# Shift and scale of the first block: dot products on VectorE replaced by TensorE products with row blocks of w_ada

## The chip, the cores and the metric

The kernel runs on one core of a Trainium2 chip. The metric is the device time of one execution in microseconds (us). Three runs of the kernel before gave 1245.27 us (median; lowest 1242.26, highest 1246.87). One further execution was profiled; it took 1246.47 us, of which 1244.7 us are the span from the first to the last recorded instruction, and the rows below come from it.

## The reference

Two transformer blocks run one after the other on 256 tokens of width 1024, all in float32. Only the start of the first block is touched here:

```python
c_act = jax.nn.silu(c)                       # c: 1 x 1024
mod = c_act @ w_ada[l] + b_ada[l]            # 6144 numbers
shift1, scale1, gate1, shift2, scale2, gate2 = jnp.split(mod, 6, axis=-1)

h = modulate(x, norm_mix_g[l], shift1, scale1)   # rmsnorm(x, g) * (1 + scale1) + shift1
proj = h @ w_in[l]                               # 256 x 1024 times 1024 x 4096
```

So `shift1` and `scale1` are the first 2048 columns of `c_act @ w_ada`, and no product with `w_in` can start before some of them are known. After that come attention, a pooling mixer, a merge, the expert layer (16 experts of each of 8 heads gathered per token from two tables of 16384 rows) and a second block with two attentions and a gated feed-forward layer. None of these is changed.

## The kernel before

**Layout.** Activations of the first stage are kept feature-major: `xT` is 128 partitions x 8 feature blocks x 256 tokens. A weight passes through `Weights` (lines 28 to 85): a list of 512 KB blocks in the order in which they are used, read by SyncE's queue into a ring of seven `raw` buffers, and, where the block is marked for it, split by ScalarE (`hi`, line 53) and VectorE (`lo`, line 54) into two parts, of which six are kept. `mm3` (line 138) makes one float32 product from three TensorE products of the parts (lines 139 to 141). A read of a new block into the ring waits until the buffer's last reader is done.

**The order.** The program is written out by hand: each engine executes its instructions in the order in which the code issues them. `FIRST` names six column groups of `w_in` whose products are made in two rounds, `g = 0` with the features 0 to 511 and `g = 1` with 512 to 1023, so that the first round needs shift and scale of half the features only. Each round has 6 blocks and 144 matmuls.

**The first phase.** `c` is read twice, as a column (`c_col`) and broadcast to all partitions (`c_all`, line 278). The host hands in `w_ada_t`, the transposed first 2048 columns of `w_ada`. `mod_dot` (line 391) takes 128 rows of it, and VectorE multiplies them by `c_all` and adds up along the row (line 394): one instruction of 1024 columns gives 128 numbers of shift or scale as one column of `modc`. Eight dots precede each round. Meanwhile ScalarE squares `xT` (line 388), TensorE adds the squares (line 307), ScalarE and VectorE make the reciprocal root (312, 313), TensorE spreads it over the partitions (316), and VectorE multiplies `xT` by it to `xn` (486). The bias is added (488), `A1 = (1 + scale) * g` is formed (489), and `affine_split` (430) makes `hh` on ScalarE (434) and `hl` on VectorE (435, 428), the two parts of `h`. Between the rounds `keep_clock` (143) issues 14 matmuls that nobody reads.

**Later columns.** The other 4096 columns of `w_ada` are already made on TensorE, spread over the following stage: `modulation` (398) multiplies `c_rep` (c in 32 equal columns) by row blocks, four column groups in four 32-row strips of one bank (line 407), and `mod_columns` (416) turns the resulting rows into columns by transposes (419).

Of the kernel before, what the change touches and what calls it, by code (L numbers as in the profile page):

```python
# [7 lines left out]
F32 = mybir.dt.float32  # L8
# [100 lines left out]
def fused_blocks_kernel(ctx: ExitStack, tc: tile.TileContext, a, out: bass.AP):  # L109
# [10 lines left out]
    def slot3(tag, name, a_, dt=F32):  # L120
        return slot(tag, name, dt).rearrange("p (a b) -> p a b", a=a_)
# [42 lines left out]
    def add_dot(n):  # L164
        W["dot", n] = block(a["w_ada_t"][n * 128:(n + 1) * 128].rearrange("p (o f) -> p o f", o=1), (1, 1024), False)
# [11 lines left out]
    for g in range(2):  # L177
        for kc in range(4 * g, 4 * g + 4):
            add_dot(8 + kc)
            add_dot(kc)  # L180
        for j in FIRST:
            in_block(j, g)
# [93 lines left out]
    ada_buf = slot3("A", "ada_buf", 2)  # L276
    c_all, ada_out = ada_buf[:, 0], ada_buf[:, 1]
    nc.sync.dma_start(c_all, a["c"].to_broadcast([128, D]))
    xT = slot3("B", "xT", KC)
    nc.sync.dma_start(xT, a["x_t"])  # L280
    vcol = const.tile([128, 76], F32, name="vcol")
    nc.sync.dma_start(vcol, a["cols1"])
    ws.prefetch(6)
    ident = const.tile([128, 128], F32, name="ident")
    nc.scalar.dma_start(ident, a["ident"])
    es = ExitStack()
# [10 lines left out]
    nc.scalar.activation(ada_out, c_all, AF.Sigmoid)  # L297
    nc.vector.tensor_tensor(c_all, c_all, ada_out, op=OP.mult)
    nc.scalar.activation(c_col[:, 1], c_col[:, 0], AF.Sigmoid)
    G_MIX, P_SCALE, G_FFN, G_FIN = 48, 56, 60, 68  # L300
# [87 lines left out]
    nc.scalar.activation(sq, xT, AF.Square)  # L388
    xn = slot3("F", "xn", KC)

    def mod_dot(n):

        w = ws.get(W["dot", n], 1)
        nc.vector.scalar_tensor_tensor(ada_out, w[:, 0], 1.0, c_all, op0=OP.mult, op1=OP.mult, accum_out=modc[:, n:n + 1])
# [3 lines left out]
    def modulation():  # L398

        for g in (1, 2):  # L400
            mp = pp.tile([128, 512], F32, tag="o", name="mp")
            for kc in range(KC):
                for half in range(2):
# [10 lines left out]
                    yield  # L414

# [39 lines left out]
    h_parts = parts(hh, hl)  # L455
    first_ps = [mm_tile(), mm_tile()] + [pp.tile([128, 512], F32, tag=tag, name="first_ps", bufs=bufs)
# [18 lines left out]

    for g in range(2):
        ks = slice(4 * g, 4 * g + 4)
        for kc in range(4 * g, 4 * g + 4):
            mod_dot(8 + kc)
            mod_dot(kc)  # L480
            if kc == 2:
                sq_ps = aux_tile()
                square_sums(sq_ps, sq, range(KC))
                rs = rstd_rows(sq_ps, rstd)
            if kc in (3, 4):
                nc.vector.tensor_tensor(xn[:, ks], xT[:, ks], rs[:, None, :].to_broadcast([128, 4, 256]), op=OP.mult)
        for c0 in (4 * g, 8 + 4 * g):
            nc.vector.tensor_tensor(modc[:, c0:c0 + 4], modc[:, c0:c0 + 4], vcol[:, c0:c0 + 4], op=OP.add)
        nc.vector.scalar_tensor_tensor(A1[:, ks], modc[:, 8 + 4 * g:12 + 4 * g], 1.0,
                                       vcol[:, G_MIX + 4 * g:G_MIX + 4 * g + 4], op0=OP.add, op1=OP.mult)  # L490
# [807 lines left out]
```

## Time and profile before

| | us |
|---|---|
| median of three runs | 1245.27 |
| the profiled execution | 1246.47 |
| its span | 1244.7 |
| TensorE busy in the span | 1064.2 (86%) |
| VectorE busy | 845.4 (68%) |
| ScalarE busy | 462.0 (37%) |
| GpSimd busy | 536.0 (43%) |

The share of an engine is an average over stages with different limits. From about 220 to 880 us gathers of the expert rows fill the transfers at some 409 GB/s; before that and after it TensorE is busy almost without a break. The change lies in the first 65 us, so the reading has to be made there. "Granted clock" is the share of the full TensorE clock as the profile gives it for a stretch; how fast the engine really steps is seen from the distance between the starts of equal matmuls.

### The profile page before, as it was taken

Reading aid. Unit: us, or ns where it says so; the run is one execution under the profiler, and the core shown is the slowest. Engines: PE = TensorE matmul, PEld = TensorE weight load, DVE = VectorE, ACT = ScalarE, POOL = GpSimd, SP = SyncE. Lnnn points to the kernel's source line nnn. Section 1 sums busy time; section 2 is a strip of 40 time slices with the busy share of each in tenths; the row PEclk is TensorE's granted clock in tenths of the full one; section 3 lists DMA queues with packets and bytes.
Section 4 is the critical chain, followed back from the end, with each engine's and each line's share of the span. In section 5 each row is a group of like instructions: output and inputs, shape, how many; then the busy total and the mean of one; then the engine's idle time right before and its main releaser. Section 6 shows DMA issues by size and latency. Waiting matters only on the chain.

```text
span 1244.7 us, 15745 instructions
## 1 busy us (share of the span) xinstructions
PE 1064.2 (86%) x5328; PEld 707.2 (57%) x5328; DVE 845.4 (68%) x1846; ACT 462.0 (37%) x887; POOL 536.0 (43%) x569
## 2 busy tenths in 40 slices
PE   4999999698889978776877777777899989999996
PEld 4977899554444423222322222222388879999995
DVE  6864475886876677668766776674356568777776
ACT  4345544323333322221322212221246464655552
POOL 0111001667677777677677777777511310000001
PEclk9999999799999999999999999999999999999998
DMA  9998984799999999999999999999986453656530
GB/s 346 330 315 307 321 284 153 278 346 406 409 386 392 407 408 409 409 409 409 358 409 409 409 409 409 409 409 409 347 289 185 153 186 123 197 181 194 183 123 34
DMA packets 161104, 390.59 MB, mean 314 GB/s; under 512 B 12472, under 2 KB 83648, under 8 KB 160768
## 3 DMA queue, kind: packets, MB, share of 16 engines
q0 software_dynamic: 74864, 272.27, 55.6%
q1 hardware_dynamic: 85520, 116.33, 28.4%
q8 instruction: 43, 0.70, 0.2%
q10 hardware_dynamic: 640, 0.98, 0.2%
q14 instruction: 37, 0.30, 0.1%
HBM read 388.22 MB, written 1.06 MB: 313 GB/s over the span
## 4 chain that ended last, share of the span: by engine, by line
PE 37%; DMA 27%; DVE 12%; POOL 9%; issue 9%; ACT 4%; SPq 0%; DVEq 0%; POOLq 0%; ACTq 0%
DMA urows<-in_peer_u_dram,ex 19%; PE mm L139 7%; PE mm L141 7%; PE mm L140 7%; DMA vrows<-in_peer_v_dram,ex 5%; POOL vrows L806 5%; DVE dot L905 5%; POOL urows L806 5%; PE acc L919 3%; PE down L141 2%; PE down L139 2%; PE down L140 2%; DVE lo L54 1%; PE mp L407 1%; ACT hi L53 1%
## 5 line engine op out<-in xcount | busy, mean ns | idle before, releaser
L919 PE MATMUL acc<-vrows,dg 128*128 128x512 f32 x1024 | 491.5, 612 | 127.9 <-ACT dg L916 89.6
L905 DVE SCALAR_TENSOR_TENSOR dot<-urows,h2rows 128x1024 f32<-128x1024 f32 x256 | 312.0, 1219 | 173.7 <-DMA urows<-in_peer_u_dram,ex 172.3
L919 PEld LDWEIGHTS acc<-vrows,dg 128*128 128x128 f32 x1024 | 178.8, 190 | 420.7 <-issue 228.6
L806 POOL DMA_INDIRECT vrows<-in_peer_v_dram,ex x256 | 242.6, 948 | 103.8 <-issue 60.5
L806 POOL DMA_INDIRECT urows<-in_peer_u_dram,ex x256 | 241.7, 944 | 93.2 <-issue 65.4
L54 DVE TENSOR_TENSOR lo<-raw,hi 128x1024 fp32r<-128x1024 f32 (+1 forms) x152 | 182.0, 1222 | 89.6 <-ACT hi L53 88.0
L916 ACT ACTIVATE dg<-ident,wgt 128x128 f32<-128x128 f32 x256 | 96.0, 397 | 252.2 <-PE acc L919 246.7
L53 ACT CAST hi<-raw 128x1024 fp32r<-128x1024 f32 (+1 forms) x152 | 154.0, 1045 | 34.1 <-DMA raw<-in_w_in_dram 25.8
L139 PE MATMUL mm<-xh,hi 128*128 128x256 f32 x480 | 137.0, 285 | 2.2 <-ACT vab L1021 2.2
L140 PE MATMUL mm<-xl,hi 128*128 128x256 f32 x480 | 136.7, 285 | 0.0
L141 PE MATMUL mm<-xh,lo 128*128 128x256 f32 x480 | 135.6, 283 | 0.0
L139 PEld LDWEIGHTS mm<-xh,hi 128*128 128x128 f32 x480 | 91.1, 190 | 5.1 <-ACT vab L1021 2.5
L140 PEld LDWEIGHTS mm<-xl,hi 128*128 128x128 f32 x480 | 91.1, 190 | 0.4
L141 PEld LDWEIGHTS mm<-xh,lo 128*128 128x128 f32 x480 | 91.3, 190 | 0.0
L1120 POOL TENSOR_TENSOR r<-r,ln 128x512 f32<-128x512 f32 x2 | 3.0, 1488 | 195.2 <-ACT r L1119 195.2
L1176 DVE SCALAR_TENSOR_TENSOR u<-mm,col,u 128x255 f32<-128x255 f32 x88 | 42.4, 482 | 33.7 <-ACT u L1173 32.1
L337 POOL TENSOR_SCALAR p<-p,mnsm 128x128 f32<-128x128 f32 (+1 forms) x24 | 20.2, 851 | 91.1 <-DVE mnsm L335 79.2
L139 PE MATMUL mm<-hh,hi 128*128 128x256 f32 x160 | 47.6, 298 | 5.2 <-ACT hi L53 5.2
L852 POOL TENSOR_TENSOR h2T<-xT,rs 128x1024 f32<-128x1024 f32 x2 | 4.7, 2352 | 107.2 <-ACT rs L847 107.2
L1173 ACT ACTIVATE u<-mm,col 128x256 f32<-128x256 f32 x44 | 24.9, 566 | 59.1 <-PE mm L141 32.4
L141 PE MATMUL mm<-hh,lo 128*128 128x256 f32 x160 | 46.3, 289 | 0.5 <-DVE lo L54 0.5
L930 ACT ACTIVATE wgt<-act 128x8 f32<-128x8 f32 x32 | 6.6, 208 | 106.8 <-DVE dot L905 106.7
(345 smaller groups left out, 1778.5 us busy)
## 6 DMA issues: line engine op xcount, KB each, us to landing
raw<-in_w_in_dram SPq DMA_DIRECT2D x45, 512.0 KB, 6.0
raw<-in_w_up_dram SPq DMA_DIRECT2D x44, 512.0 KB, 4.3
raw<-in_w_ada_dram SPq DMA_DIRECT2D x32, 512.0 KB, 5.2
raw<-in_w_down_dram SPq DMA_DIRECT2D x22, 512.0 KB, 4.0
raw<-in_w_ada_t_dram SPq DMA_DIRECT2D x16, 512.0 KB, 8.2
raw<-in_w_out_dram SPq DMA_DIRECT2D x16, 512.0 KB, 4.9
raw<-in_peer_wq_dram SPq DMA_DIRECT2D x8, 512.0 KB, 5.6
urows<-in_peer_u_dram,ex POOLq DMA_INDIRECT x256, 8.0
```

The lines of the kernel that those rows point to most:

```text
L53: self.nc.scalar.copy(hi, raw)
L54: self.nc.vector.tensor_tensor(lo, raw, hi.bitcast(F32), op=OP.subtract)
L139: nc.tensor.matmul(o, lh, rh, start=first, stop=False)
L140: nc.tensor.matmul(o, lh, rl, start=False, stop=False)
L141: nc.tensor.matmul(o, ll, rh, start=False, stop=last)
L337: eng.tensor_scalar(neg[:, s], neg[:, s], sm[:, i:i + 1], None, op0=OP.mult)
L806: nc.gpsimd.indirect_dma_start(out=g, out_offset=None, in_=tables[kind], in_offset=bass.IndirectOffsetOnAxis(ap=experts[unit][:, k:k + 1], ...
L905: nc.vector.scalar_tensor_tensor(dot, u, 1.0, h2rows, op0=OP.mult, op1=OP.mult, accum_out=act[:, half * HK + k:half * HK + k + 1])
L916: nc.scalar.activation(dg, ident, AF.Copy, scale=wgts[prev][:, k:k + 1])
L919: nc.tensor.matmul(acc[:, s], dg, v[:, s], start=prev == ((prev[0][0], 0), 0) and k == 0, stop=prev == ((prev[0][0], NH - 1), 1) and k == ...
L1173: nc.scalar.activation(dst, src, AF.Identity, bias=ccol[:, 3, c + f:c + f + 1], scale=ccol[:, 2, c + f:c + f + 1])
L1176: nc.vector.scalar_tensor_tensor(dst[:, n:], src[:, :256 - n], ccol[:, 2 - n, c + f:c + f + 1], dst[:, n:], op0=OP.mult, op1=OP.add)
```

## The change

Shift and scale of the first block are made the way the later columns were: `first_products` multiplies `c_rep` by row blocks of `w_ada` itself. A block holds 128 rows of `w_ada` and, for one half of the features, 512 columns of shift and 512 of scale; its two matmuls go to two 32-row strips of one bank, and eight blocks add up to the result for a half. `first_columns` copies the two strips out, turns them into columns by four transposes, adds the bias and forms `A1`. The first half's products stand ahead of round 0, mixed with the sums of squares; the second half's stand inside round 0, behind the groups 4, 5 and 6. `c` is no longer broadcast by a read; `c_rep` is made at the start on GpSimd. `x` is read and squared in two halves. `vcol` and `ident` are read by ScalarE's queue. Ahead of round 1 there are 5 unread matmuls in place of 14.

```diff
+    def add_first_ada(g, kc):
+
+        rows = a["w_ada"][0][kc * 128:(kc + 1) * 128, 0:2048].rearrange("p (o h f) -> p o h f", o=2, h=2)
+        W["ada", 0, kc, g] = block(rows[:, :, g], (2, 512), False)
...
     for g in range(2):
-        for kc in range(4 * g, 4 * g + 4):
-            add_dot(8 + kc)
-            add_dot(kc)
+        for kc in range(KC):
+            add_first_ada(g, kc)
         for j in FIRST:
             in_block(j, g)
...
-    ada_buf = slot3("A", "ada_buf", 2)
-    c_all, ada_out = ada_buf[:, 0], ada_buf[:, 1]
-    nc.sync.dma_start(c_all, a["c"].to_broadcast([128, D]))
     xT = slot3("B", "xT", KC)
-    nc.sync.dma_start(xT, a["x_t"])
-    vcol = const.tile([128, 76], F32, name="vcol")
-    nc.sync.dma_start(vcol, a["cols1"])
-    ws.prefetch(6)
+    x_halves = slice(0, 4), slice(4, 8)
+    for ks in x_halves:
+        nc.sync.dma_start(xT[:, ks], a["x_t"][:, ks])
...
+    ws.prefetch(7)
...
-    nc.scalar.activation(ada_out, c_all, AF.Sigmoid)
-    nc.vector.tensor_tensor(c_all, c_all, ada_out, op=OP.mult)
     nc.scalar.activation(c_col[:, 1], c_col[:, 0], AF.Sigmoid)
+    nc.vector.tensor_tensor(c_col[:, 0], c_col[:, 0], c_col[:, 1], op=OP.mult)
+    c_rep = tmp.tile([128, KC, 32], F32, name="c_rep", bufs=1)
+    nc.gpsimd.tensor_copy(c_rep, c_col[:, 0, :, None].to_broadcast([128, KC, 32]))
...
-    nc.scalar.activation(sq, xT, AF.Square)
+    for ks in x_halves:
+        nc.scalar.activation(sq[:, ks], xT[:, ks], AF.Square)
...
+    def first_products(g, mp, kcs):
+
+        for kc in kcs:
+            w = ws.get(W["ada", 0, kc, g], 1)
+            for j in range(2):
+                nc.tensor.matmul(mp[32 * j:32 * j + 32, :], c_rep[:, kc, :], w[:, j, :],
+                                 start=kc == 0, stop=kc == KC - 1, tile_position=(0, 32 * j))
+
+    def first_columns(g, mp, mt):
+
+        row = tmp.tile([128, 512], F32, tag="modrow", name="modrow", bufs=1)[0:64]
+        nc.vector.tensor_copy(row, mp[0:64])
+        for b in range(4):
+            nc.tensor.transpose(mt[:, b * 64:(b + 1) * 64], row[:, b * 128:(b + 1) * 128], ident[0:64, 0:64])
...
+        nc.vector.tensor_tensor(both, v, vcol[:, 0:16].rearrange("p (j b) -> p j b", j=2)[:, :, ks], op=OP.add)
+        nc.vector.scalar_tensor_tensor(A1[:, ks], modc[:, 8 + 4 * g:12 + 4 * g], 1.0,
+                                       vcol[:, G_MIX + 4 * g:G_MIX + 4 * g + 4], op0=OP.add, op1=OP.mult)
...
+    sq_ps, first_mp = aux_tile("sums"), aux_tile("first_mp")
+    square_sums(sq_ps, sq, range(0, 4))
+    first_products(0, first_mp, range(0, 3))
+    square_sums(sq_ps, sq, range(4, 8))
+    first_products(0, first_mp, range(3, 6))
+    rs = rstd_rows(sq_ps, rstd)
+    first_products(0, first_mp, range(6, KC))
+    first_columns(0, first_mp, pp.tile([128, 512], F32, tag="s", name="mt", bufs=2))
+    for ks in x_halves:
+        nc.vector.tensor_tensor(xn[:, ks], xT[:, ks], rs[:, None, :].to_broadcast([128, 4, 256]), op=OP.mult)
...
+    first_mp = aux_tile("first_mp")
+    FIRST_ADA = {4: (0, 1, 2), 5: (3, 4, 5), 6: (6, 7)}
     for g in range(2):
         ks = slice(4 * g, 4 * g + 4)
-        for kc in range(4 * g, 4 * g + 4):
-            mod_dot(8 + kc)
-            mod_dot(kc)
-            if kc == 2:
-                sq_ps = aux_tile()
-                square_sums(sq_ps, sq, range(KC))
-                rs = rstd_rows(sq_ps, rstd)
-            if kc in (3, 4):
-                nc.vector.tensor_tensor(xn[:, ks], xT[:, ks], rs[:, None, :].to_broadcast([128, 4, 256]), op=OP.mult)
...
-            nc.vector.tensor_tensor(c_col[:, 0], c_col[:, 0], c_col[:, 1], op=OP.mult)
-            c_rep = tmp.tile([128, KC, 32], F32, name="c_rep", bufs=1)
-            nc.vector.tensor_copy(c_rep, c_col[:, 0, :, None].to_broadcast([128, KC, 32]))
...
+            if g == 0 and j in FIRST_ADA:
+                first_products(1, first_mp, FIRST_ADA[j])
+                if j == 6:
+                    first_columns(1, first_mp, aux_tile("mt"))
             if g == 0 and j == FIRST[-1]:
-                keep_clock(aux_tile(), hh, 14)
+                keep_clock(aux_tile(), hh, 5)
```

On TensorE the start of the program reads so, before (-) and now (+). `aux` and `sums` hold the sums of squares, `first_mp` the products with `w_ada` (two matmuls for a block), `mt` the transposes.

```order
-L307 MATMUL aux<-ones,sq 128x1 x16
-L316 MATMUL aux<-ident,rstd 128x128 x2
+L308 MATMUL sums<-ones,sq 128x1 x8
+L418 MATMUL first_mp<-raw,c_rep 32x512 x6
+L308 MATMUL sums<-ones,sq 128x1 x8
+L418 MATMUL first_mp<-raw,c_rep 32x512 x6
+L317 MATMUL sums<-ident,rstd 128x128 x2
+L418 MATMUL first_mp<-raw,c_rep 32x512 x4
+L426 MATMUL mt<-ident,modrow 128x64 x4
```

Sixteen matmuls and four transposes have come to stand between the sums and the first product with `w_in`, and the second half of the sums now stands behind the first six of them.

On VectorE, around the first use of `A1` (shown as `A_113`), the program before has these rows; `ada_buf` is written by the dots.

```order
L394 SCALAR_TENSOR_TENSOR ada_buf,modc<-raw,ada_buf 128x1024 x6
L313 RECIPROCAL rstd<-rstd 128x2
L394 SCALAR_TENSOR_TENSOR ada_buf,modc<-raw,ada_buf 128x1024 x2
L486 TENSOR_TENSOR xn<-xT,aux 128x1024
L488 TENSOR_TENSOR modc<-modc,vcol 128x4 x2
L489 SCALAR_TENSOR_TENSOR A_113<-modc,vcol 128x4
L435 TENSOR_SCALAR mtmp<-xn,A_113,modc 128x256 x2
```

The changed program has these at the same place (`A1` is `A_116`); `modrow` is the copy of the two strips.

```order
L314 RECIPROCAL rstd<-rstd 128x2
L424 COPY modrow<-first_mp 64x512
L430 TENSOR_TENSOR modc<-mt,vcol 128x2x4
L431 SCALAR_TENSOR_TENSOR A_116<-modc,vcol 128x4
L483 TENSOR_TENSOR xn<-xT,sums 128x1024 x2
L453 TENSOR_SCALAR mtmp<-xn,A_116,modc 128x256 x2
```

The dots are gone, and both halves of `xn` now stand behind `A1`, where one half stood ahead of it.

On TensorE inside and behind round 0, the second half's last block and the transposes stand between the groups 6 and 7, and the unread matmuls are fewer.

```order
 L140 MATMUL first_ps<-lo,hh 128x256
 L141 MATMUL first_ps<-hi,hl 128x256
+L418 MATMUL first_mp<-raw,c_rep 32x512 x4
+L426 MATMUL mt<-ident,modrow 128x64 x4
 L139 MATMUL first_ps<-hi,hh 128x256
...
-L146 MATMUL aux<-hh 128x512 x14
+L146 MATMUL aux<-hh 128x512 x5
```

Two more groups of six such matmuls (not shown) stand behind the groups 4 and 5.

## Rows read from the trace of the kernel before

**Rows 1.** Who TensorE waited for from 24 to 216 us (total, times, longest).

```profile
PE mm L139 <- ACT hi L53: 5.2, 1, 5.2
PE mp L407 <- DVE modrow L411: 1.2, 1, 1.2
```

**Rows 2.** Timeline, 19 to 25 us: start, duration, engine, line, operation.

```profile
19.21 1.22 DVE L394 SCALAR_TENSOR_TENSOR ada_buf<-raw,ada_buf 128x1024 f32<-128x1024 f32 x1
...
20.36 1.22 DVE L486 TENSOR_TENSOR xn<-xT,aux 128x1024 f32<-128x1024 f32 x1
21.50 0.23 DVE L488 TENSOR_TENSOR modc<-modc,vcol 128x4 f32<-128x4 f32 x2
21.76 0.16 DVE L489 SCALAR_TENSOR_TENSOR A<-modc,vcol 128x4 f32<-128x4 f32 x1
21.95 0.60 ACT L434 ACTIVATE hh<-xn,modc,A 128x256 fp32r<-128x256 f32 x1 [4.12 <-DVE A L489]
...
24.50 1.23 DVE L54 TENSOR_TENSOR lo<-raw,hi 128x1024 fp32r<-128x1024 f32 x1 [0.70 <-ACT hi L53]
```

**Rows 3.** Timeline of TensorE, 24 to 31 us.

```profile
24.52 0.58 PE L139 MATMUL mm<-hh,hi 128*128 128x256 f32 x1 [5.22 <-ACT hi L53]
...
25.79 0.58 PE L141 MATMUL mm<-hh,lo 128*128 128x256 f32 x1 [0.47 <-DVE lo L54]
...
30.43 0.41 PE L141 MATMUL mm<-hh,lo 128*128 128x256 f32 x1
...
30.80 0.28 PE L140 MATMUL mm<-hl,hi 128*128 128x256 f32 x1
```

**Rows 4.** Timeline of TensorE, 40 to 64 us: the end of round 0.

```profile
44.94 3.38 PE L146 MATMUL aux<-hh 128*128 128x512 f32 x14
48.15 0.28 PE L139 MATMUL mm<-hh,hi 128*128 128x256 f32 x1
```

**Rows 5.** Timeline, 8 to 11 us.

```profile
8.58 1.91 ACT L388 ACTIVATE sq<-xT 128x2048 f32<-128x2048 f32 x1 [1.38 <-DMA xT<-in_x_t_dram]
```

**Rows 6.** Stages: length; busy PE, PEld, DVE, ACT, POOL; granted clock, DMA share, GB/s.

```profile
10.00:18.00 8.00, 6.99 (x32) 6.90 (x32) 7.54 (x14) 2.04 (x3) 0.00 (x0) 1.00 1.02 411
18.00:24.00 6.00, 1.22 (x4) 0.93 (x4) 5.66 (x14) 2.04 (x4) 0.00 (x0) 1.00 1.09 349
24.50:30.60 6.10, 5.61 (x24) 5.32 (x25) 6.09 (x8) 5.21 (x6) 0.00 (x0) 1.00 1.07 384
```

**Rows 7.** Timeline of TensorE, 10 to 19 us: the sums of squares and the spread.

```profile
10.54 6.99 PE L307 MATMUL aux<-ones,sq 128*128 128x1 f32 x32 [10.54 <-ACT sq L388]
18.08 1.22 PE L316 MATMUL aux<-ident,rstd 128*128 128x128 f32 x4 [0.55 <-DVE rstd L313]
```

**Rows 8.** Timeline of TensorE, 210 to 262 us: sums, transposes and products with wq.

```profile
210.54 0.94 PE L307 MATMUL sq_ps<-ones,sq 128*128 128x1 f32 x8
...
218.56 3.44 PE L795 MATMUL h2rows<-ident,h2T 128*128 128x128 f32 x7 [0.16 <-ACT h2T L854]
...
222.01 0.42 PE L140 MATMUL mm<-xal,hi 128*128 128x258 f32 x1
...
225.37 0.28 PE L141 MATMUL mm<-xah,lo 128*128 128x258 f32 x1
...
234.89 2.08 PE L688 MATMUL sp<-keyT,qv 128*128 128x128 f32 x8 [5.64 <-ACT qv L672]
```

**Rows 9.** Timeline of TensorE, 108 to 120 us, without the mm3 products.

```profile
113.66 1.05 PE L407 MATMUL mp<-raw,c_rep 128*32 128x512 f32 x4
114.64 0.66 PE L419 MATMUL mt<-ident,modrow 128*128 128x128 f32 x4
115.23 1.05 PE L407 MATMUL mp<-raw,c_rep 128*32 128x512 f32 x4
```

**Rows 10.** Timeline of VectorE, 107 to 119 us: the copy of four strips.

```profile
108.09 0.69 DVE L411 COPY modrow<-mp 128x512 f32<-128x512 f32 x1
```

More of the change, by code (lines that the diff above doesn't have):

```diff
@@ L162, in cols @@
         W[key] = [block(src[:, k:k + 4], (4, n)) for k in range(0, w.shape[0] // 128, 4)]
-    def add_dot(n):
-        W["dot", n] = block(a["w_ada_t"][n * 128:(n + 1) * 128].rearrange("p (o f) -> p o f", o=1), (1, 1024), False)
+    def add_first_ada(g, kc):
+        rows = a["w_ada"][0][kc * 128:(kc + 1) * 128, 0:2048].rearrange("p (o h f) -> p o h f", o=2, h=2)
+        W["ada", 0, kc, g] = block(rows[:, :, g], (2, 512), False)
     def add_ada(g, kc, half):
@@ L275, in fused_blocks_kernel @@
     nc.sync.dma_start(c_col[:, 0], a["c_t"])
-    ada_buf = slot3("A", "ada_buf", 2)
-    c_all, ada_out = ada_buf[:, 0], ada_buf[:, 1]
-    nc.sync.dma_start(c_all, a["c"].to_broadcast([128, D]))
     xT = slot3("B", "xT", KC)
-    nc.sync.dma_start(xT, a["x_t"])
-    vcol = const.tile([128, 76], F32, name="vcol")
-    nc.sync.dma_start(vcol, a["cols1"])
-    ws.prefetch(6)
+    x_halves = slice(0, 4), slice(4, 8)
+    for ks in x_halves:
+        nc.sync.dma_start(xT[:, ks], a["x_t"][:, ks])
     ident = const.tile([128, 128], F32, name="ident")
     nc.scalar.dma_start(ident, a["ident"])
+    vcol = const.tile([128, 76], F32, name="vcol")
+    nc.scalar.dma_start(vcol, a["cols1"])
+    ws.prefetch(7)
     es = ExitStack()
@@ L387, in fused_blocks_kernel @@
     rstd = const.tile([128, 2], F32, name="rstd")
-    nc.scalar.activation(sq, xT, AF.Square)
+    for ks in x_halves:
+        nc.scalar.activation(sq[:, ks], xT[:, ks], AF.Square)
     xn = slot3("F", "xn", KC)
-    def mod_dot(n):
-        w = ws.get(W["dot", n], 1)
-        nc.vector.scalar_tensor_tensor(ada_out, w[:, 0], 1.0, c_all, op0=OP.mult, op1=OP.mult, accum_out=modc[:, n:n + 1])
     mod_row = {}
@@ L414, in modulation @@
                     yield
+    def first_products(g, mp, kcs):
[9 more added lines that the diff above has]
+            nc.tensor.transpose(mt[:, b * 64:(b + 1) * 64], row[:, b * 128:(b + 1) * 128], ident[0:64, 0:64])
+        v = mt[:, 0:256].rearrange("p (b j r) -> p j b r", b=4, j=2)[:, :, :, 0]
+        ks = slice(4 * g, 4 * g + 4)
+        both = modc[:, 0:16].rearrange("p (j b) -> p j b", j=2)[:, :, ks]
+        nc.vector.tensor_tensor(both, v, vcol[:, 0:16].rearrange("p (j b) -> p j b", j=2)[:, :, ks], op=OP.add)
+        nc.vector.scalar_tensor_tensor(A1[:, ks], modc[:, 8 + 4 * g:12 + 4 * g], 1.0,
+                                       vcol[:, G_MIX + 4 * g:G_MIX + 4 * g + 4], op0=OP.add, op1=OP.mult)
     def mod_columns(g):
@@ L474, in rope @@
         nc.vector.tensor_tensor(dst, dst, t, op=OP.add)
+    first_mp = aux_tile("first_mp")
+    FIRST_ADA = {4: (0, 1, 2), 5: (3, 4, 5), 6: (6, 7)}
     for g in range(2):
         ks = slice(4 * g, 4 * g + 4)
-        for kc in range(4 * g, 4 * g + 4):
-            mod_dot(8 + kc)
-            mod_dot(kc)
-            if kc == 2:
-                sq_ps = aux_tile()
-                square_sums(sq_ps, sq, range(KC))
-                rs = rstd_rows(sq_ps, rstd)
-            if kc in (3, 4):
-                nc.vector.tensor_tensor(xn[:, ks], xT[:, ks], rs[:, None, :].to_broadcast([128, 4, 256]), op=OP.mult)
[L487 to L490, printed above, removed]
         if g == 1:
```

## The prediction

> **What bounds the kernel now.** I read the waits of TensorE first, over the stretch from its first product with `w_in` to the expert layer. It waits once for long, 5.2 us for the first `hi`; every later wait is 1.2 us or less [rows 1]. So from about 25 to 216 us the end is set by TensorE's own work, and what comes later or is added there moves everything behind it, the gathers too. Two things then decide: when round 0 gets going, and how long TensorE needs from there to round 1.
>
> *When.* The dense start of round 0 is 25.79 us, where the first `lo` arrives; the two matmuls before it only fill a gap [rows 3]. I call this point D. Going back, the timeline has the last dot at 19.21, half of `xn` at 20.36, the bias at 21.50, `A1` at 21.76, `hh` at 21.95 and `lo` at 24.50 [rows 2]. VectorE had been idle for 0.70 us before that `lo`, so ScalarE's chain (`hh`, `hi`) ended last.
>
> *How long.* Round 0 runs from D to 44.94, then 14 unread matmuls fill 3.21 us until round 1 at 48.15 [rows 4], or 0.23 us each. The first part steps at half speed: between the rows at 25.79 and 30.43 matmuls of 256 columns last 0.41 us and start 0.21 us apart (22 of them in 4.64 us), from 30.80 on they last 0.28 us and start 0.12 us apart [rows 3]. [...] The half-speed stretch from 24.52 to 30.6 costs about 3 us.
>
> **The change part by part, ahead of round 0.** P is the end of the eighth pair of products.
>
> *Transfers.* Reads run at 411 GB/s where a row piece is 4 KB, at 349 where `w_in` pieces of 1 KB are read [rows 6]. Without the broadcast of `c` (0.52 MB) the eighth block, which the last dot used at 19.21, can be there about 1.3 us earlier, at some 17.9. The new pieces have 2 KB; between the two rates this is 0 to 1.8 us more for eight blocks of 0.52 MB. I take 18.5. [...]
>
> *Sums.* `x` was squared from 8.58 on [rows 5]. Half of `x` without the broadcast is 1.05 MB less, 2.55 us: 6.0. Half the squares take 0.95 us, so the sums start at about 7.0. All sums together take 6.99 us [rows 7] without getting faster, so half of them 3.5 us, to 10.5. (At full speed eight records start in 0.8 to 0.94 us [rows 8], so half the sums are 1.8 us.) `c_rep`, a copy of 256 columns on GpSimd, has until 10.5 and costs nothing; without that cover a copy of this kind would add about the 0.7 us that one of 512 columns takes on VectorE [rows 10], or a few times that on GpSimd. `vcol` and `ident`, now on ScalarE's queue ahead of its first activation, are needed only behind P.
>
> *Pairs.* [...] Whether such pairs raise the clock no row shows. Dense streams of full matmuls got the full pace 6.1 us after 24.52 [rows 3] and 3.4 us after 222.0 [rows 8]; I take 4.9 us after 10.5, that is 15.4. Then two and a half of the first three pairs are done, the third ends at 15.9, the second half of the sums at 17.7, three pairs at 20.6, the spread of the root (1.22 us at half speed [rows 7]) at 21.2, two pairs at 23.2. So P = 23.2: TensorE is behind the transfers, and these stop mattering.
>
> *From P to D.* The copy takes 0.69 us [rows 10], four transposes at most 0.59 at full speed [rows 9], say 0.7, the bias 0.26 to `A1`, and 0.15 for three hand-overs: 1.8 us. From the start of `A1` to D it was 4.03 us [rows 2, 3]. Now two halves of `xn` at 1.14 us stand in between on VectorE; its slack of 0.70 us covers part: 4.03 + 2.28 - 0.70 = 5.6. D = P + 7.4 = 30.6, which is 4.8 us later than 25.79. TensorE stands nearly idle between P and D, so it starts round 0 at half speed again, as after 5.64 us of idling at 234.89 [rows 8], and the 3 us are not gained.
>
> **Inside round 0.** The dots of the second half ran on VectorE beside round 0 and cost only the 3.21 us of filling. Now eight pairs stand in TensorE's own stream: 8 x 0.98 = 7.8 us. Behind the last of them TensorE waits for the copy (0.8 us) and makes the transposes (0.6 us). Then 24 matmuls (2.8 us) and 5 unread ones (1.15 us) run while bias, `A1`, `hh`, `hi` and `lo` are made, 4.3 us: 0.35 us of waiting. Sum: 7.8 + 0.8 + 0.6 + 1.15 + 0.35 - 3.2 = +7.5 us. VectorE has lost the 8 dots there and is free for the copy.
>
> The reads do not hold round 1 up: the ring now waits for TensorE's pairs, but the first block of round 1 is asked for when the second pair is done, some 15 us ahead of use.
>
> **Sum.** 4.8 + 7.5 = 12.3 us. From 1246.47 us of the profiled execution that is 1258.8; the median of the runs lies 1.2 us lower, which gives 1257.6. I put 1257.
>
> **Rivals.**
>
> *The clock never rises before round 0.* Pairs on 64 of 128 columns and sums, which left the clock low for 7 us [rows 7], might not raise it. Then the pairs take 1.96 us each: 10.5 + 5.9 + 3.5 + 5.9 + 1.2 + 3.9 = 30.9 = P, D = 38.3, together +20 us: 1265. For it speaks the row of the sums, against it that pairs stream 512 columns each without a break.
>
> *Not slower: the clock is high from the first sums on and stays so through round 0.* TensorE now works from 7 us on almost without a gap until P. Then sums and pairs take 1.8 + 2.9 + 1.8 + 2.9 + 0.6 + 2.0 = 12 us after 7.0, P = 19.0, D = 26.4, +0.6; round 0 loses its half-speed stretch, -3.05; with +7.5 this is +5.0: 1250.3, within what can be told from no change. It decides from where the first `w_in` triples start 0.12 us apart instead of 0.21. Against it speak the 7 us of sums at half speed [rows 7], and that seven transposes in 3.44 us did not keep the pace: the products behind them ran at 0.42 us [rows 8]. [...]
>
> *The end is not TensorE's.* If the stretch behind were paced by transfers, lateness would be absorbed. All waits after the first are short [rows 1], so at most some 2 us of the 12 would go: 1255. A real gain would need round 0 to begin several us ahead of 25.79 in spite of the 18 us that the transfers alone take; P + 7.4 does not allow it.
>
> **How the numbers follow.** The forecast and its near variants (pairs at 0.9, rise a little earlier or later, 1252 to 1261) get 0.57, the low clock 0.17, the high clock 0.12, absorption 0.08, and 0.06 is left for a gain that I do not see. 0.5% is 6.2 us, about what can be told apart here; slower starts at 1251.5. The low clock, the forecast and most of absorption lie above, less the low edge of the forecast: 0.73; the high clock and these edges are the same, 0.21; faster 0.06. The range, 1248 to 1265, takes in the high clock's 1250 and the low clock's 1265; alone, the forecast's would be 1252 to 1261.
>
> **What would show it.** In the changed profile: the eighth pair ends between 21 and 25 us; D is about 7.4 us behind it with both halves of `xn` behind `A1`; the first triples of round 0 at 0.21 us; pairs of about 1 us inside round 0; one gap of 0.8 us before the transposes; round 1 at about 60 us instead of 48.15, and the expert layer later by the same. It would be wrong if round 1 started before 53 us, or if it started late and the expert layer did not.

## The result and the profile after

The changed kernel took 1252.45 us (median of five runs, 1250.81 to 1254.64) against 1245.27 us (five runs, 1242.26 to 1247.12): ratio 1.0057, 95% interval 1.0041 to 1.0073, which is 7.2 us slower (5.1 to 9.1). The profiled execution took 1250.81 us, the lowest of its five, with a span of 1249.0 us. TensorE is busy for 10.3 us more and VectorE for 18.7 us less, as the page's first part says (busy time, share of the span, instructions; before 1064.2 us of PE and 845.4 us of DVE).

```profile
span 1249.0 us, 15827 instructions
...
PE 1074.5 (86%) x5391; PEld 705.0 (56%) x5391; DVE 826.7 (66%) x1812; ACT 461.4 (37%) x887; POOL 539.8 (43%) x570
```

The first phase, from the timeline of the changed kernel (start, duration, engine, line, operation, and in brackets the idle time before it with what ended it):

```profile
6.36 3.57 PE L308 MATMUL sums<-ones,sq 128*128 128x1 f32 x16 [6.36 <-ACT sq L390]
...
9.86 5.28 PE L418 MATMUL first_mp<-raw,c_rep 128*32 128x512 f32 x12
15.07 1.95 PE L308 MATMUL sums<-ones,sq 128*128 128x1 f32 x16
16.95 2.77 PE L418 MATMUL first_mp<-raw,c_rep 128*32 128x512 f32 x12
...
19.64 0.71 PE L317 MATMUL sums<-ident,rstd 128*128 128x128 f32 x4
20.29 1.91 PE L418 MATMUL first_mp<-raw,c_rep 128*32 128x512 f32 x8
22.24 0.68 DVE L424 COPY modrow<-first_mp 64x512 f32<-64x512 f32 x1 [4.73 <-PE first_mp L418]
22.98 0.46 PE L426 MATMUL mt<-ident,modrow 64*128 64x64 f32 x4 [0.79 <-DVE modrow L424]
...
23.76 2.35 DVE L483 TENSOR_TENSOR xn<-xT,sums 128x1024 f32<-128x1024 f32 x2
```

The first half of the sums takes 3.57 us and the second 1.95: between them the pace rose from half to full, beside three pairs that took 5.28 us where the next three took 2.77. (The granted clock reads 1.00 from 6.3 to 22.3 us, at either pace.) P, the end of the eighth pair, is 20.29 + 1.91 = 22.2. Then TensorE, from 24 us to past the start of round 0; these rows answer to [rows 3]:

```profile
27.58 0.58 PE L139 MATMUL mm<-hh,hi 128*128 128x256 f32 x1 [4.14 <-ACT hi L53]
...
29.06 0.58 PE L141 MATMUL mm<-hh,lo 128*128 128x256 f32 x1 [0.68 <-DVE lo L54]
...
32.00 0.30 PE L139 MATMUL mm<-hh,hi 128*128 128x256 f32 x1
```

D is 29.06, 3.3 us later than before, and round 0 again begins at half pace (products 0.21 us apart; the granted clock reads 0.50 from 27.5 to 32 us and 1.00 from 32 to 36, but in the kernel before it reads 1.00 at half pace too [rows 6], so the pace decides), but only for 2.9 us from D (to 32.00), where it was 4.9 us from 25.79 to the first faster product of the kernel before:

```profile
30.64 0.31 PE L139 MATMUL mm<-hh,hi 128*128 128x256 f32 x1
```

The second half's eight pairs and the transposes follow inside round 0; the last two rows answer to [rows 4]:

```profile
38.88 2.77 PE L418 MATMUL first_mp<-raw,c_rep 128*32 128x512 f32 x12
...
44.68 2.77 PE L418 MATMUL first_mp<-raw,c_rep 128*32 128x512 f32 x12
...
50.41 1.91 PE L418 MATMUL first_mp<-raw,c_rep 128*32 128x512 f32 x8
...
53.11 0.46 PE L426 MATMUL mt<-ident,modrow 64*128 64x64 f32 x4 [0.79 <-DVE modrow L424]
...
56.48 1.32 PE L146 MATMUL aux<-hh 128*128 128x512 f32 x5
57.63 0.28 PE L139 MATMUL mm<-hh,hi 128*128 128x256 f32 x1
```

Round 1 begins at 57.63 instead of 48.15, 9.5 us later: 3.3 us ahead of D and 6.2 us inside round 0 (28.57 us from D to round 1, before 22.36). Who TensorE waited for from 20 to 225 us (total, times, longest) has the two waits for the copy of the strips (`mt`), which the change itself puts there, and one entry that the kernel before has nowhere, `sc` (a product of the attention scores) for VectorE's `qk`:

```profile
PE mm L139 <- ACT hi L53: 4.1, 1, 4.1
PE mt L426 <- DVE modrow L424: 1.6, 2, 0.8
PE sc L353 <- DVE qk L502: 1.4, 1, 1.4
PE mp L404 <- DVE modrow L408: 1.2, 1, 1.2
PE mm L141 <- DVE lo L54: 0.7, 1, 0.7
```

The rotated copies of `qk` (`qk_turned`) are made by small transfers right behind round 1's first products. After the change these are issued at 64.40 and VectorE uses the first at 72.79, 8.4 us later; before they were issued at 54.90 and used at 61.48, 6.6 us later. First VectorE's row of the kernel before, then of the changed one:

```profile
61.48 0.69 DVE L472 TENSOR_TENSOR qk_turned<-qk_turned,rope_c 128x512 f32<-128x512 f32 x1 [4.54 <-DMA qk_turned<-qk_raw]
```

```profile
72.79 0.69 DVE L500 TENSOR_TENSOR qk_turned<-qk_turned,rope_c 128x512 f32<-128x512 f32 x1 [7.20 <-DMA qk_turned<-qk_raw]
```

The gathers of the expert layer (GpSimd's issues of `urows`: their number, min/median/max of one, first and last start) began at 232.4 us, 10.0 us later than the 222.4 of before, and their last one came at 887.6, 6.9 us later than 880.7. So in these two profiles the stage of the gathers is 3.1 us shorter after the change (655.2 against 658.3 us), and behind it another 2.6 us go: the span ends 4.3 us later. (The medians lie 7.2 us apart, these two profiled executions only 4.3 us: 1246.47 and 1250.81 us.)

```profile
L824 POOL DMA_INDIRECT urows<-in_peer_u_dram,ex x256: 932/941/1406, 232.4 to 887.6; - x128
```

So two questions are left for experiments: what of the 9.5 us each part of the change costs, and whether lateness at round 1 reaches the end whole (the forecast) or the later stages give a part of it back (its rival). The kernel before was profiled twice more for this; both profiles are of slowed executions, so only their rows up to the first gather are read.

### The profile page after: what moved, and what is told of

Its sections match the earlier page's. It is cut to its first block, busy times and chain, and to the rows that moved or that the text cites. A ratio compares the mean times of both kernels' runs of the same rounds, so it can differ in the third digit from the quotient of the medians.

```text
span 1249.0 us, 15827 instructions
## 1 busy us (share of the span) xinstructions
PE 1074.5 (86%) x5391; PEld 705.0 (56%) x5391; DVE 826.7 (66%) x1812; ACT 461.4 (37%) x887; POOL 539.8 (43%) x570
## 4 chain that ended last, share of the span: by engine, by line
PE 39%; DMA 20%; POOL 14%; issue 13%; DVE 10%; ACT 3%; SPq 0%; POOLq 0%; DVEq 0%; ACTq 0%
DMA urows<-in_peer_u_dram,ex 12%; PE mm L139 8%; PE mm L141 8%; PE mm L140 8%; POOL vrows L824 7%; POOL urows L824 7%; DMA vrows<-in_peer_v_dram,ex 5%; DVE dot L923 3%; PE acc L937 3%; PE down L141 2%; PE down L139 2%; PE down L140 2%; DVE lo L54 1%; PE first_mp L418 1%; PE mp L404 1%
## 5 line engine op out<-in xcount | busy, mean ns | idle before, releaser
L140 PE MATMUL mm<-hl,hi 128*128 128x256 f32 x160 | 45.8, 286 | 0.0
```

Of the source, the lines that this page charges most:

```text
L140: nc.tensor.matmul(o, lh, rl, start=False, stop=False)
```

## The experiments

The first four kernels ran on one chip, where the kernel before took 1245.77 us (median of 25). The other eight ran on two further chips, where the gathers moved 335 to 366 GB/s in five of their profiles (in two stretches of 325 us each) instead of 397 to 407; the kernel before took 1334 and 1335 us there. Of those runs I use ratios and the profiles up to the first gather. Percentages are turned into us with the time of before on the same chip.

**Lateness alone.** In the kernel before, 40 more unread matmuls ahead of round 1.

```diff
             if g == 0 and j == FIRST[-1]:
-                keep_clock(aux_tile(), hh, 14)
+                keep_clock(aux_tile(), hh, 54)
```

> The kernel before with 54 instead of 14 unread matmuls ahead of round 1, that is 40 x 0.23 us = 9.2 us of pure lateness from round 1 on, about as much as the changed kernel has there (57.63 against 48.15, +9.5). Theory A (TensorE sets the end and lateness passes on whole; the smaller difference at the end of the changed kernel is scatter of the gather stage): round 1 at 57.4, first gather about 9 us later, time +8 to +10 us, 1253 to 1255. Theory B (a later stage gives part of it back whatever the kernel): first gather +9, but the time only +5 to +7 us, 1250 to 1252, and the gather stage 2 to 4 us shorter than before's 658.

Measured: 1250.85 us, ratio 1.0042 (95% interval 1.0027 to 1.0057, as in all that follow), +5.2 us (3.4 to 7.1). TensorE's timeline and the gathers' issues of this kernel:

```profile
44.45 12.44 PE L146 MATMUL aux<-hh 128*128 128x512 f32 x54
56.73 0.28 PE L139 MATMUL mm<-hh,hi 128*128 128x256 f32 x1
```

```profile
L806 POOL DMA_INDIRECT urows<-in_peer_u_dram,ex x256: 932/937/1808, 229.3 to 884.3; - x128
```

Round 1 is 8.6 us late, the gathers 6.9 us, the time 5.2 us. By itself this looks like a give-back on the way, with nothing of the change in the kernel. Note also that no `sc` waits for `qk` here.

**Group 1 by dots again.** The changed kernel with only the first half's shift and scale on TensorE.

```diff
-            add_first_ada(g, kc)
+            if g == 0:
+                add_first_ada(g, kc)
+            elif kc >= 4:
+                add_dot(8 + kc)
+                add_dot(kc)
...
         if g == 1:
+            nc.vector.tensor_tensor(c_all, c_all, ada_out, op=OP.mult)
+            for kc in range(4, 8):
+                mod_dot(8 + kc)
+                mod_dot(kc)
...
-            if g == 0 and j in FIRST_ADA:
-                first_products(1, first_mp, FIRST_ADA[j])
...
-                keep_clock(aux_tile(), hh, 5)
+                keep_clock(aux_tile(), hh, 14)
```

> The changed kernel with the second half undone: shift and scale of features 512 to 1023 again from eight dots on VectorE beside round 0 (c broadcast read behind the first seven blocks), 14 unread matmuls. Theory A (the eight pairs in TensorE's stream cost 6 us, the later start of round 0 3 us): D stays at about 29, round 1 starts 22 us after it, at 51 instead of 57.6; time about 6 us below the changed kernel, 1246 to 1248. Rival (the pairs in round 0 only fill what the reads would have left idle anyway, since now the reads wait for TensorE): round 1 stays near 56 to 58 and the time near 1252.

Measured: 1246.94 us, ratio 1.0009 (0.9990 to 1.0028), +1.1 us (-1.2 to +3.5). Round 1 begins so:

```profile
51.51 0.28 PE L139 MATMUL mm<-hh,hi 128*128 128x256 f32 x1
```

Round 1 is 6.1 us earlier than in the changed kernel, and the time is 6.1 us less (7.2 - 1.1, with some 3 us to either side by the two intervals). So the second half's pairs, which stand in TensorE's own stream, are most of the loss. What the first half's cost is less sure: +1.1 us in the time, inside the interval, but round 1 is still 3.4 us later than before.

**Full pace from the first sums.** The changed kernel with four unread products at its start.

```diff
     h_parts = parts(hh, hl)
+    unread = aux_tile("unread")
+    for _ in range(4):
+        nc.tensor.matmul(unread, ones, ones[:, None, :].to_broadcast([128, 4, 128]), start=True, stop=True)
     sq_ps, first_mp = aux_tile("sums"), aux_tile("first_mp")
```

> The changed kernel with four unread 512-column matmuls on the constant ones at the start, before the first sums. Theory A (the half-speed pairs and sums made P late): first sums or first pairs already at full pace, the first three pairs take 2.7 us instead of 5.2, P comes at 18.5 to 20 instead of 22.2, D at 25.5 to 27, round 1 at 54 to 55.5, time 2.5 to 3.5 us below the changed kernel, 1249 to 1250. Rival (the reads of w_ada end last): P stays at 21 to 22 and nothing moves.

Measured: 1250.12 us, ratio 1.0033 (1.0021 to 1.0045), +4.1 us (2.6 to 5.6). TensorE's timeline:

```profile
7.37 1.84 PE L308 MATMUL sums<-ones,sq 128*128 128x1 f32 x16
...
11.34 1.05 PE L418 MATMUL first_mp<-raw,c_rep 128*32 128x512 f32 x4 [0.29 <-DMA raw<-in_w_ada_dram]
...
17.54 1.91 PE L418 MATMUL first_mp<-raw,c_rep 128*32 128x512 f32 x8
...
26.31 0.58 PE L141 MATMUL mm<-hh,lo 128*128 128x256 f32 x1 [0.68 <-DVE lo L54]
...
55.42 0.28 PE L139 MATMUL mm<-hh,hi 128*128 128x256 f32 x1
```

The first sums go at full pace (1.84 us for 16), P is 19.45, 2.75 us earlier, D 2.75, round 1 2.2. But behind P TensorE waited 4.1 us for `hi`, and round 0 starts at 0.58 and 0.41 us per matmul, half pace again. So the rival "high clock" needs more than full pace ahead of P. One pair now waited for its block, 0.29 us: with the pairs this early the reads are nearly what ends last.

**Both `xn` ahead of the copy.** In the changed kernel the spread of the root moves behind the fourth pair, and both halves of `xn` ahead of the copy of `modrow`.

```diff
-    first_products(0, first_mp, range(3, 6))
+    first_products(0, first_mp, range(3, 4))
     rs = rstd_rows(sq_ps, rstd)
-    first_products(0, first_mp, range(6, KC))
-    first_columns(0, first_mp, pp.tile([128, 512], F32, tag="s", name="mt", bufs=2))
     for ks in x_halves:
         nc.vector.tensor_tensor(xn[:, ks], xT[:, ks], rs[:, None, :].to_broadcast([128, 4, 256]), op=OP.mult)
+    first_products(0, first_mp, range(4, KC))
+    first_columns(0, first_mp, pp.tile([128, 512], F32, tag="s", name="mt", bufs=2))
```

> The changed kernel with the spread of the root behind the fourth pair and both halves of xn ahead of the copy of the strips on VectorE. Theory A (xn behind A1 made D 1.4 us later): P unchanged at 22.2, A1 at 23.7, D at 27.7 instead of 29.06, round 1 at about 56.3; time 1 to 1.5 us lower, 1251, which is near the limit of what can be told. Rival (hi of the first w_in block ends last whatever xn does): D stays at 29.

Measured: 1249.86 us, ratio 1.0038 (1.0022 to 1.0054), +4.7 us (2.7 to 6.7). TensorE's timeline:

```profile
9.76 4.22 PE L418 MATMUL first_mp<-raw,c_rep 128*32 128x512 f32 x12
...
17.41 3.63 PE L418 MATMUL first_mp<-raw,c_rep 128*32 128x512 f32 x16
21.82 0.46 PE L426 MATMUL mt<-ident,modrow 64*128 64x64 f32 x4 [0.79 <-DVE modrow L424]
25.29 0.38 PE L139 MATMUL mm<-hh,hi 128*128 128x256 f32 x1 [3.00 <-ACT hi L53]
...
26.55 0.58 PE L141 MATMUL mm<-hh,lo 128*128 128x256 f32 x1 [0.76 <-DVE lo L54]
...
55.13 0.28 PE L139 MATMUL mm<-hh,hi 128*128 128x256 f32 x1
```

From the transposes to D it is 4.73 us, in the changed kernel 6.08: what VectorE's `xn` cost behind P is 1.35 us, not the 2.28 - 0.70 = 1.58 us of the forecast. The other 1.16 us at D are not the edit's: P is 21.04 instead of 22.20, and the difference is there before the edit's place is reached, since the first three pairs, beside which the pace rose, took 4.22 us here and 5.28 us there (4.83 in the changed kernel's second profile). Round 1 is 2.5 us earlier than after the change, the time 2.5 us less (7.2 - 4.7).

**The kernel before once more, and three tests of the give-back.** First the same kernel again, for the scatter of a single profile:

> The kernel before once more, unchanged, for the scatter of what is read from one profile. In its first profile the stretch from the first to the last row fetched by the gathers took 658.3 us, against 654.9 to 656.2 in the five kernels that reach it later, and the granted clock fell for some microseconds behind the gathers (0.82 and 0.84 in the two 5 us from 915), which three of the five do not show. If these belong to the kernel (a gather stage reached earlier is longer, and the clock falls behind it), this profile shows 658 us and the fall again. If they are scatter of one execution, the stretch comes out near 655 to 657 and part of the 3 us that the late kernels seemed to win back there was never there. The time is that of before, ratio 1.000, in either case.

Ratio 0.9998 (0.9957 to 1.0039). Round 1 began at 48.21 us, 0.06 us off the first profile; the first gather came at 224.1 instead of 222.4. What it was made for it could not tell: the gathers ran at 335 and 354 GB/s here (235 to 560 and 560 to 885 us), so the length of the gather stage compares with nothing.

Then twice the lateness, 94 unread matmuls instead of 54:

> The kernel before with 94 unread products ahead of round 1 where it has 14: 80 more of 0.2304 us are 18.4 us of pure lateness at round 1 (66.6 instead of 48.15), twice that of the run with 54, which came out 5.1 us slower (3.4 to 6.7). If a fixed few microseconds are given back later (5.1 of 9.2 kept: 4.1 lost once), the time is 18.4 - 4.1 = 14.3 us above before: 1260. If a share is given back (5.1/9.2 = 0.55 kept), it is 10.2 us above: 1256. If nothing is given back and the first run was low, 18.4 us: 1264.

Ratio 1.0126 (1.0054 to 1.0198), +16.8 us (7.2 to 26.4): too wide to tell. Round 1 at 66.06, first gather at 239.9.

Then the same 40 matmuls as in the first delay, but just ahead of the gathers:

```diff
     first_queries.run()
+    keep_clock(pp.tile([128, 1024], F32, tag="h2", name="unread")[:, 0:512], xah[:, :, 0:256], 40)
     square_sums(sq_ps, sq2, (6, 7))
```

> The kernel before with 40 unread products of 512 columns (9.2 us at 0.2304 us) put on TensorE just ahead of the gathers, between the first query products and the sums for rstd at 210.5. The lateness begins at 210 instead of 45, and the rounds in between run as in before. If the give-back lies between round 1 and the gathers (transfers that were waited for at 57 to 210), all of it is kept: about +9.2 us, 1255. If it lies in the gather stage and behind it, as the milestones of the profiles say, the time is that of the run with the 40 products at 45: +5 us (3.5 to 6.5), 1251.

Ratio 1.0060 (1.0019 to 1.0100), +8.0 us (2.5 to 13.3): again both fit. Both were run a second time, on the third chip:

> The 9.2 us ahead of the gathers again, on another occasion, since the gathers of the first time moved 350 GB/s instead of 409 and its interval (+2.5 to +13 us) held both theories. There the first gather came at 232.5, 8.4 to 10.1 us later than in the two profiles of before, so the lateness is whole when the gathers begin. If about 2.6 us are given back once, in the gather stage or behind it, whatever the lateness, the time is +6 to +7 us (1.005); if nothing is given back there, +9 us (1.0074).

> The 18.4 us at round 1 again, for the same reason (first time +7 to +26 us; first gather at 239.9, 15.8 to 17.5 later than before). A fixed loss behind the gathers of 2.6 us (the mean of the five late kernels so far: 2.8, 1.8, 3.2, 3.6, 1.8) gives +14 to +15 us (1.0115); a share of 0.55 to 0.72 kept gives +9 to +12 us (1.008 to 1.010); no give-back gives +16 to +17.5 (1.0135).

The delay ahead of the gathers gave 1.0108 (1.0073 to 1.0143), +14.4 us (9.7 to 19.1); the 18.4 us at round 1 gave 1.0123 (1.0089 to 1.0157), +16.4 us (11.9 to 21.0). If a share of 0.55 of the lateness were kept, that would be +10 us for the latter and +5 for the former: both intervals exclude that. The first reading of the delay run, that about half of the lateness is given back, falls. A share of 0.72, which the expectation names too, would be +13 us for the 18.4, and that interval holds it. A fixed loss of some 2 us fits the 18.4 us as well as no loss; the delay ahead of the gathers shows no loss at all, its interval even begins above the 9.2 us that were put in.

The changed kernel once more:

> The changed kernel once more, unchanged, for a second ratio and a second profile of it. Ratio 1.0041 to 1.0073 as the first time where the gathers move some 400 GB/s; P, D and round 1 at 22.2, 29.06 and 57.6 within 0.2 us, first gather at 232 to 234. If the gather stage is 655 us again and the granted clock stays at 1.00 behind the gathers, the two are the late kernel's own; if not, they are scatter of one execution.

Ratio 1.0052 (1.0023 to 1.0081), +6.9 us (3.1 to 10.8). P is 21.87 and D 28.73, but the pace in round 0 rose later: half pace until 34.66, 5.9 us from D, where the first profile had 2.9.

```profile
34.45 0.38 PE L140 MATMUL mm<-hl,hi 128*128 128x256 f32 x1
34.66 0.29 PE L141 MATMUL mm<-hh,lo 128*128 128x256 f32 x1
...
58.56 0.28 PE L139 MATMUL mm<-hh,hi 128*128 128x256 f32 x1
```

Round 1 is at 58.56, 0.9 us later in spite of the earlier D, and the first gather at 234.3. I had expected P, D and round 1 within 0.2 us and the first gather by 234, and all four missed: P and D because the pace rose earlier beside the pairs (4.83 us for the first three), round 1 because it rose later in round 0. And the kernel before a third time:

> The kernel before, unchanged, for a third profile of it beside the three late kernels of this call. If the give-back is real, its stretch from the first to the last row fetched is 658 us as in the first profile, 2 to 3 us more than in the late kernels of this call, or its clock falls behind the gathers where theirs does not. If it was scatter of the first profile, it is at 655 to 657 like theirs, and the clock falls or not without regard to the kernel. Ratio 1.000.

Ratio 0.9993 (0.9962 to 1.0024). Round 1 began at 47.80 and the first gather came at 226.0. The gathers were slow on this chip too (343 and 359 GB/s in the changed kernel's second profile), so whether the gather stage of the kernel before is really 658 us, or its one profile had a long one, stays open.

**All that helped, together.** Only the first half by pairs, unread products at the start, both `xn` early, and three unread products behind the first transposes:

```diff
+    for _ in range(4):
+        nc.tensor.matmul(unread, ones, ones[:, None, :].to_broadcast([128, 4, 128]), start=True, stop=True)
...
-    first_products(0, first_mp, range(3, 6))
+    first_products(0, first_mp, range(3, 4))
...
+    first_products(0, first_mp, range(4, KC))
+    first_columns(0, first_mp, pp.tile([128, 512], F32, tag="s", name="mt", bufs=2))
+    unread = aux_tile("unread")
+    for _ in range(3):
+        nc.tensor.matmul(unread, ones, ones[:, None, :].to_broadcast([128, 4, 128]), start=True, stop=True)
```

> Changed kernel with four edits together: only group 0's shift and scale by TensorE products, group 1's by dots on VectorE as in before; four unread fp32 products at the start, so that sums and pairs run at full pace (that alone brought D, the first product of round 0, from 29.06 to 26.31); both xn ahead of the copy of modrow and part of the group 0 pairs behind them (that alone D 26.55); three unread products behind the first transposes and 14 before round 1. If the two gains at D add up, D is 24 to 24.5 and round 1 is at 44 to 46.5, ahead of before's 48.15 by 2 to 4 us, and the time is 1242 to 1244.5 if the lead is kept, 1244 to 1245 if half of it is given back later as with lateness. If the copies, transposes and xn bound D anyway (both edits win the same 2.7 us), D stays at 26.3, round 1 at 47 to 49 and the time at that of before, 1245 to 1246.5.

Measured: ratio 0.9997 (0.9966 to 1.0029), no better than before. TensorE's timeline:

```profile
15.64 4.92 PE L433 MATMUL first_mp<-raw,c_rep 128*32 128x512 f32 x16
...
24.82 0.38 PE L139 MATMUL mm<-hh,hi 128*128 128x256 f32 x1 [0.23 <-ACT hi L53]
...
26.08 0.39 PE L141 MATMUL mm<-hh,lo 128*128 128x256 f32 x1 [0.76 <-DVE lo L54]
...
43.11 3.37 PE L146 MATMUL aux<-hh 128*128 128x512 f32 x14
...
47.06 0.39 PE L139 MATMUL mm<-hh,hi 128*128 128x256 f32 x1 [0.58 <-ACT hi L53]
...
48.32 0.39 PE L141 MATMUL mm<-hh,lo 128*128 128x256 f32 x1 [0.76 <-DVE lo L54]
```

Here the pace stays full through round 0 (0.38 and 0.28 us per matmul from the first), and round 0 is done by 43.11. But D is 26.08, near the rival's 26.4, though not for its reason. From the transposes to D it is 4.72 us, as with `xn` first; P, however, is 20.6 where the warm start alone had 19.45, because the clock fell once more behind the spread of the root: the granted clock reads 0.50 from 15.5 to 18 us, and the last four pairs took 4.92 us instead of 3.63 (with `xn` first alone). One window shows it (length; busy PE, PEld, DVE, ACT, POOL; granted clock, DMA share, GB/s):

```profile
15.50:17.00 1.50, 1.50 (x5) 0.37 (x6) 1.25 (x2) 0.00 (x0) 0.00 (x0) 0.50 1.00 391
```

And the lead at 43.11 is lost ahead of round 1, whose first product waits for ScalarE's `hi` and whose third, the first that needs `lo`, waits for VectorE until 48.32. Behind this wait stand the dots, which this kernel has on VectorE again. First the kernel before, then this one (the last dot and the first `lo`):

```profile
42.20 1.22 DVE L394 SCALAR_TENSOR_TENSOR ada_buf<-raw,ada_buf 128x1024 f32<-128x1024 f32 x1
...
46.49 1.23 DVE L54 TENSOR_TENSOR lo<-raw,hi 128x1024 fp32r<-128x1024 f32 x1 [0.70 <-ACT hi L53]
```

```profile
42.74 1.23 DVE L406 SCALAR_TENSOR_TENSOR ada_buf<-raw,ada_buf 128x1024 f32<-128x1024 f32 x1
...
47.04 1.23 DVE L54 TENSOR_TENSOR lo<-raw,hi 128x1024 fp32r<-128x1024 f32 x1 [0.70 <-ACT hi L53]
```

In the kernel before this chain ends at 47.72, and the third product of round 1 starts at 48.38: VectorE had less than 1 us of slack there (it was busy for 19.05 of the 20 us from 20 to 40). Here the chain ends at 48.27. So with the dots on VectorE the first `lo` of round 1 is ready some 22 us behind D (25.79 to 47.72 there, 26.08 to 48.27 here), whatever TensorE gains inside round 0. Whether the four edits are any better than the dots alone (ratio 1.0009) their intervals do not tell.

## Why the prediction was right, and where it was off

Direction and mechanism were right: slower, because TensorE is what bounds this stretch (its waits behind the first are 1.2 us or less [rows 1]), and 16 pairs came into its stream for dots that VectorE had made beside it. VectorE was nearly full there (19.05 of the 20 us from 20 to 40), but what it did cost TensorE only the 3.2 us of filling, as the prediction says. The size was off: forecast +11.7 us, measured +7.2. By the steps:

- *Sums and transfers: right.* The sums were to start at 7.0 and half of them to end at 10.5; they started at 6.36 and the pairs at 9.86. `c_rep` took GpSimd 0.40 us, less than either price that the forecast names for such a copy. (In the profile of before GpSimd takes 1.09 us for a TENSOR_SCALAR of 128x256 and VectorE 0.41, 2.7 times.) The pairs never waited for a transfer, so the forecast's 18.5 was not tested by this kernel; in the warm one, whose pairs come earlier, one waited 0.29 us, and the reads moved 387 GB/s from 10 to 15 us, between the forecast's two rates.
- *The rise of the clock: right, by the pace.* It was to rise at about 15.4, beside the pairs; the sums at 15.07 are the first at full pace. So the pace rose behind 3.57 us of sums and 5.28 us of pairs, where 6.99 us of sums alone had left the spread behind them at 1.22 us [rows 7], against 0.71 here. The rival "the clock never rises" is out.
- *The pairs: a little too dear.* 0.98 us was taken from a pair that stood alone [rows 9]; in a row they take 0.92 (2.77 us for three). No run shows the 1.96 us for a pair at half pace, which the forecast uses up to the rise of the clock and the low clock's 1265 throughout: it was my estimate, twice the 0.98. The first three pairs here start 1.70 us apart. P is 22.2 instead of 23.2: 0.64 us of that is the earlier start, the pairs give most of the rest.
- *P to D: right within the step, 6.9 instead of 7.4 us.* The copy, 0.79 of waiting, the transposes and both `xn` are there in that order. D is 29.06 instead of 30.6, +3.3 instead of +4.8.
- *Half pace again at round 0: right, but for 2.9 us instead of 4.9, so 1 us was gained after all.* This was luck: in the second profile of the same kernel it is 5.9 us, and the 1 us is lost again. The forecast treated the length of that stretch as fixed; in five profiles of kernels that are the same as before up to there it runs from 3.3 to 5.1 us. It also priced the stretch at 3 us, counted from 24.52, when TensorE still waited; without it round 0 took 17.03 us from D in the kernel with all four edits, against 19.15 before, so 2.1 us. What lets the pace fall ahead of round 0 was not shown: no run separates the transposes from the waiting behind them. With 4.1 us of waiting the first product is at 0.58 us, with 3.0 us (`xn` first) it is at 0.38, and with three unread products behind the transposes and 0.23 us of waiting it is at 0.38 too and stays there.
- *Inside round 0: +7.5 forecast, +6.2 and, in the second profile, +7.5 measured* (29.83 us from D to round 1, less 22.36). Of its terms the eight pairs took 2.77 + 2.77 + 1.91 = 7.45 instead of 7.8 us, the wait for the copy 0.79 as forecast, the transposes some 0.4 instead of 0.6, and nothing waited at round 1 instead of 0.35. Round 0's own matmuls took 18.93 us from D instead of 19.15: the 1 us from the earlier full pace is mostly spent again, as each group behind pairs or transposes runs a little longer than before (24 matmuls in 3.0 to 3.1 us instead of 2.8 to 2.9).
- *Round 1 at about 60: 57.6 and 58.6.* That is +9.5 and +10.4 instead of +12.3. So 2 to 3 of the 4.5 us of error had been made by here, in terms that were sized from single rows.
- *"All waits after the first are short" and the rest follows 1:1: one wait was missed.* TensorE's `sc` now waits 1.3 to 1.6 us for `qk`. It does so in the four kernels in which the second half's shift and scale are made by pairs (the changed one twice, the warm one, the one with `xn` first) and in none of the ten profiles of the other kernels, which have dots there. Its releaser is a chain from `qk_turned`, whose transfers took 8.4 us (changed) and 8.8 us (`xn` first) from issue to use, against 6.6 us before and 5.6 us with 40 unread more. Why they took longer was not tried.
- *Lateness reaches the end: borne out by the differences among the late kernels, open for 2 us against before.* The table has round 1, first gather, and the time against before on the same chip (95% interval).

| kernel | round 1 | first gather | time, us |
|---|---|---|---|
| before | 48.15 | 222.4 | |
| changed | 57.63 | 232.4 | +7.2 (5.1 to 9.1) |
| changed, again | 58.56 | 234.3 | +6.9 (3.1 to 10.8) |
| group 1 by dots | 51.51 | 225.3 | +1.1 (-1.2 to 3.5) |
| warm start | 55.42 | 230.0 | +4.1 (2.6 to 5.6) |
| `xn` first | 55.13 | 230.1 | +4.7 (2.7 to 6.7) |
| 40 unread more | 56.73 | 229.3 | +5.2 (3.4 to 7.1) |
| 80 unread more | 66.06, 66.11 | 239.9, 240.3 | +16.8 (7.2 to 26.4), +16.4 (11.9 to 21.0) |
| 40 unread ahead of the gathers | 48.88, 47.35 | 232.5, 231.9 | +8.0 (2.5 to 13.3), +14.4 (9.7 to 19.1) |
| all four | 47.06, from 48.32 without a gap | 222.4 | -0.4 (-4.5 to 3.9) |

Among the kernels of the first chip and the changed one, round 1 earlier by 6.1, 2.5 and 2.2 us made the time shorter by 6.1, 2.5 and 3.1 us: no giving back is seen. Each of these differences has some 3 us to either side, so that they agree so closely is in part chance. Against the profile of before, though, each of them comes out 1.7 to 3.5 us better than its first gather says (each with about 2 us to either side), the one that is late by 2.9 us as well as the one that is late by 10.0. On the third chip the changed kernel points the same way: round 1 at 58.56 against 47.80, 10.8 us later, for +6.9 us (3.1 to 10.8). A loss that does not grow with lateness is not a cushion that absorbs it; an offset in the one profile of before that all are compared with would look the same. Its first gather at 222.4 is one draw (224.1 and 226.0 in the two repeats, on other chips). Its gather stage is 658.3 us, those of the five others between 654.9 and 656.2. Which it is, the later chips could not show, so about 2 of the 4.5 us stay unexplained.

The rival "not slower, high clock" was wrong about this kernel. The kernel with all four edits has full pace through round 0 and comes out level with before, but it has not the second half's pairs, so it does not test the rival's sum.

## What to carry to other kernels

Work moved into the stream of the engine that bounds the stage costs its length there, less only what it saves that engine: the eight pairs with their wait and transposes put 8.5 us into TensorE's round 0 and saved it 2.1 us of unread matmuls, and undoing them won 6.1 of the 7.2 us. That VectorE was relieved of 8 dots bought no more than that. Ahead of the stage, where the bounding engine waits anyway, the same work cost less: 1.1 us in the time, not told from nothing, or 3.4 us by round 1 of one profile. With the dots in place the two engines were nearly level (VectorE's chain was ready less than 1 us ahead of TensorE's), so making TensorE alone faster inside round 0 bought nothing either: in the last experiment round 0 was done 1.8 us sooner than before, and round 1 began no sooner. And sizes read from one profile carry 1 us or more of scatter in when the pace rises and a further 2 us in long stages: compare several changed kernels with one another before calling a difference "given back".

## What was not expected of the hardware

- In two profiles of the same kernel (the changed one) the pace rose 2.9 and 5.9 us after D, in the kernels with a like start 3.2 (`xn` first), 4.2 (warm start) and 5.9 us (group 1 by dots). A product of 256 columns starts every 0.21 us before and every 0.12 us after, so the scatter is worth some 1.3 us.
- Behind 4.1 us of waiting the first product took 0.58 us and the next 0.41; behind 3.0 us of waiting (`xn` first) the first two products still ran at 0.38 and 0.28 us, and it was the next, 0.76 us of waiting later, that took 0.58.
- The chip made a difference of 7%: with the gathers at 335 to 366 GB/s instead of 397 to 407 and a mean granted clock of about 0.945 instead of 0.985, the same kernel took 1334 us instead of 1246, while its round 1 began within 0.4 us of the same time. Why these chips are slower no run here shows.
